# A hybrid decoder trunk on one core: holding the order of the output projections, dealing out the splits of y by weight tile, and moving one chunk of tokens to the second group

## The chip, the core and the metric

The kernel runs on one core of one Trainium2 chip. The core has five engines with an instruction stream each: TensorE (PE: matmuls, with weight loads shown as PEld), VectorE (DVE), ScalarE (ACT), GpSimd (POOL) and SyncE (SP), which here issues all the DMAs. An engine works through its stream in order and waits at an instruction until what it needs is there. The metric is the time of one launch in microseconds of the device, as a median over several runs.

## What is computed

Two layers of a hybrid trunk on 1040 tokens (16 meta tokens and 1024 of the sequence) of width 1024, all in float32:

```python
def hybrid_layer(x, ...):
    h = rms_norm(x, norm_g)
    z = h @ w_in                       # 1024 -> 6408, split in parts
    ya = sliding_window_sink_attention(...) * silu(ag)          # 16 heads, 2 KV heads
    ym = rms_norm(mlstm_chunkwise(...)) * sigmoid(mo) * silu(mgate)
    y = concatenate([ya, ym], -1) @ w_out                       # 2048 -> 1024
    return x + y
```

After the last layer the meta tokens are dropped.

## The kernel before

**Precision.** A float32 product is made of three matmuls in a faster format: each operand is split in a high part (`hi`, a rounded copy, made on ACT) and a low part (`lo`, the value less `hi`, made on DVE or POOL), and hi x hi, hi x lo and lo x hi are added in one PSUM bank. Weights come from DRAM into one of two `raw` buffers, and their parts go into one of the eight slots of a ring (`RING`). `wpair` (L147) does so for the input weights, `wout` (L168) for the output weights: a load on SP (L172), `hi` on ACT (L174), `lo` on DVE or POOL (L175).

**Stages of a layer.** K and V (`kv_tasks`), queries and gates woven with attention, the mLSTM heads woven with their projections, and the output projection, which ends the layer. In the first layer each finished token tile is then normalised and transposed into `H` for the next layer (`norm_tile`, L273). The order on PE is held by hand in the attention stage alone: `pin` (L65 ff.) ties a PE instruction behind the one traced before it while `in_order[0]` is true, and it is false in the output projection. Wherever it is false, and for every other engine always, the order of a stream is chosen by the scheduler at build time, from the order of tracing as priority and from simulated times; the chip then runs that fixed stream.

**The output projection** (L1087 to L1162). Its input y has 16 tiles of 128 features; 14 lie in DRAM (`spool`) and the last two made (`ym`, order positions 12 and 13) are still on chip. First a loop over all 16 tiles and all three chunks of tokens (`CH`: 272, 384 and 384 tokens) loads y (L1096) and splits it: `hi` into `H` on ACT (L1100), `lo` into `ylo` on DVE or on POOL for every third tile (L1105), and in layer 0 extra copies for the 16 meta tokens (L1102, L1103). Then four groups follow: token tiles 0 to 4 (in the last layer 1 to 4) with the left half of the columns of `w_out` and with the right half, then token tiles 5 to 8 with both halves. A group goes through the 16 weight tiles; each is multiplied with every token tile of the group (`product`, L1131), three matmuls of 512 columns each, or two for token tile 0, where 16 tokens are handled with a stacked operand. Every token tile of a group has its own PSUM bank, taken in turn from three pools with two banks each (`pj`, `pss`, `po`); a fourth pool, `pt`, also of two, takes transposes. The last group alone goes through its last eight weights tile by tile (`cut`).

When a token tile is done, DVE adds the residual out of the bank (L1153, for token tile 0 L1152 too). In the last layer the result goes to the output (L1155). In the first it is stored to `x1` in DRAM (L1157), and ACT takes the sum of its squares (L1158, whose unused result is written over the bank). After the right half, the left half is loaded back (L1161) and `norm_tile` follows: the factor on DVE and POOL (L277 to L279), the scaling on DVE (L285), eight transposes on PE (L288), and the parts into `H` on ACT and DVE (L291, L292).

**Buffers.** Loads of y alternate between the pool `p512` (4 buffers) and `t384` (5 buffers). The results, and the left halves loaded back, are in `p512` too.

Of the kernel before, what the change touches and what calls it, by code (L numbers as in the profile page):

```python
# [29 lines left out]
TT = [(0, 16)] + [(16 + 128 * i, 128) for i in range(8)]  # L30
CH = [(0, 272, range(0, 3)), (272, 384, range(3, 6)), (656, 384, range(6, 9))]
# [31 lines left out]
def build(ctx, tc, I, O):  # L63
# [4 lines left out]
    def pin(ins):  # L68

        return tc.keep_in_program_order(ins) if in_order[0] else ins  # L70
# [25 lines left out]
    def bank(tag):  # L96
        return bp[tag].tile([128, 512], F32, name=tag)
# [70 lines left out]
    def wout(l, k, c0, i):  # L168
        raw = rawp.tile([128, 2, 264], F32, name="raw").rearrange("p a b -> p (a b)")[:, 0:512]
        pair = RING[:, ring_i[0] % NPAIR]  # L170
        ring_i[0] += 1
        sy.dma_start(raw, I["w_out"][l][k * 128:(k + 1) * 128, c0:c0 + 512])  # L172
        hi, lo = [pair[:, a].rearrange("p a b -> p (a b)")[:, 0:512] for a in range(2)]
        sc.activation(hi, raw, AF.Copy)  # L174
        (ve if i % 3 == 2 else gp).tensor_tensor(lo, raw, hi, op=ALU.subtract)  # L175
        return hi, lo

    def mm3(out, pairs):
# [92 lines left out]
            done = upto  # L271


    def norm_tile(t, xh, ssq_ap, gbc):
        t0, p = TT[t]
        v = sm.tile([128, 2], F32, name="nv", bufs=2)
        ve.tensor_reduce(v[:p, 0:1], ssq_ap, axis=mybir.AxisListType.X, op=ALU.add)  # L277
        ve.tensor_scalar(v[:p, 0:1], v[:p, 0:1], 1.0 / D, EPS, ALU.mult, ALU.add)
        gp.tensor_tensor(v[:p, 1:2], v[:p, 0:1], nhalf[:p, 0:1], op=ALU.pow)  # L279
        for g in range(2):  # L280
            if gbc is None:
                ve.tensor_scalar(xh[g][:p, :], xh[g][:p, :], v[:p, 1:2], None, ALU.mult)
            for i in range(2 if gbc is not None else 0):
                xs = xh[g][:p, 256 * i:256 * i + 256]
                ve.scalar_tensor_tensor(xs, xs, v[:p, 1:2], gbc[2 * g + i][:p, 0:256], ALU.mult, ALU.mult)  # L285
            ps = bank("pt")
            for k in range(4):
                pin(pe.transpose(ps[:, k * p:(k + 1) * p], xh[g][:p, k * 128:(k + 1) * 128], ident[:p, :p]))  # L288
            src = ps[:, 0:4 * p].rearrange("p (k t) -> p k t", k=4)
            hi = H[:, 4 * g:4 * g + 4, t0:t0 + p]  # L290
            sc.activation(hi, src, AF.Copy)  # L291
            ve.tensor_tensor(H[:, 8 + 4 * g:12 + 4 * g, t0:t0 + p], src, hi, op=ALU.subtract)  # L292
            if t == 0:
                for i in range(3):
                    ve.tensor_copy(HM[:, 4 * g:4 * g + 4, 16 * i:16 * i + 16],
                                   H[:, 4 * (g + i // 2 * 2):4 * (g + i // 2 * 2) + 4, 0:16])

    def load_g(l):
        out = []
# [12 lines left out]
    def first_norm(t, xt, G):  # L312
        t0, p = TT[t]
        st = sm.tile([128, 2], F32, name="nst", bufs=2)
        xg = []
        for i in range(2):
            j = bank("pss") if i else bank("po")
            sc.activation(j[:p, :], xt[:p, 512 * i:512 * i + 512], AF.Square, accum_out=st[:p, i:i + 1])
            y = p512(F32)
            gp.tensor_tensor(y[:p, :], xt[:p, 512 * i:512 * i + 512], G[:p, 512 * i:512 * i + 512], op=ALU.mult)  # L320
            xg.append(y)
        norm_tile(t, xg, st[:p, 0:2], None)

    snk = cp.tile([128, 2, HEADS], F32, name="snk")
    qrt = cp.tile([128, 9, 32], F32, name="qrt")
# [18 lines left out]
    def parameters2(rows):  # L344
# [5 lines left out]
        for t in ptm:  # L350
            ve.tensor_scalar(t, ident, 0.0, None, ALU.mult)

    for l in range(DEPTH):
        last = l == DEPTH - 1
        first_q = 1 if last else 0
# [96 lines left out]
        def kv_tasks():  # L452
# [634 lines left out]
        order = list(range(0, 12)) + [14, 15, 12, 13]  # L1087
        s0 = N_META if last else 0
        ylo = {}
        for i, k in enumerate(order):  # L1090
            ylo[k] = unit(F32R)
            for c, (t0, n, _) in enumerate(CH):
                a = s0 if c == 0 else t0
                if k < 14:
                    y = p512(F32, t0 + n - a) if (i + c) % 2 else t384(t0 + n - a)
                    sy.dma_start(y, spool[k, :, a:t0 + n])  # L1096
                else:
                    y = ym[k - 14][:, a:t0 + n]
                hi = H[:, k, a:t0 + n]
                sc.activation(hi, y, AF.Copy)  # L1100
                if a == 0:
                    sc.activation(ylo[k][:, L:L + 32], y[:, 0:32], AF.Copy)  # L1102
                    gp.tensor_tensor(ylo[k][:, L + 32:L + 48], y[:, 0:16], ylo[k][:, L:L + 16], op=ALU.subtract)  # L1103
                eng = gp if i % 3 == 2 else ve
                eng.tensor_tensor(ylo[k][:, a:t0 + n], y, hi, op=ALU.subtract)  # L1105
# [5 lines left out]
        nb = 0  # L1111
        for grp in (range(first_q, 5), range(5, 9)):
            for hf in range(2):
                c0 = 512 * hf
                pss_t = {}
                for t in grp:
                    pss_t[t] = bank(pools[nb % 3])
                    nb += 1
                def product(i, k, t, w):
                    t0, p = TT[t]  # L1120
                    ps = pss_t[t]
                    wh, wl = w
                    if t == 0:
                        st = ylo[k][:, L:L + 48]
                        terms = ((st, wh), (st, wl))
                        p = 48
                    else:
                        hi, lo = H[:, k, t0:t0 + p], ylo[k][:, t0:t0 + p]
                        terms = ((hi, wh), (hi, wl), (lo, wh))
                    for n, (a, b) in enumerate(terms):  # L1130
                        pin(pe.matmul(ps[:p, :], a, b, start=(i + n == 0), stop=(i == 15 and n == len(terms) - 1)))  # L1131

                cut = 16 - 8 if hf == 1 and grp[-1] == 8 else 16
                for i, k in enumerate(order[:cut]):
                    w = wout(l, k, c0, i)
                    for t in grp:
                        product(i, k, t, w)
                tail = [(i, order[i], wout(l, order[i], c0, i)) for i in range(cut, 16)]
                for t in grp:
                    for i, k, w in tail:  # L1140
                        product(i, k, t, w)
                    t0, p = TT[t]
                    xr = p512(F32)
                    if l > 0:
                        src = x1[t0:t0 + p, c0:c0 + 512]
                    elif t == 0:
                        src = I["meta"][:, c0:c0 + 512]
                    else:
                        src = I["x"][t0 - 16:t0 + 112, c0:c0 + 512]
                    sy.dma_start(xr[:p, :], src)  # L1150
                    if t == 0:
                        ve.tensor_tensor(xr[:16, :], pss_t[t][32:48, :], xr[:16, :], op=ALU.add)  # L1152
                    ve.tensor_tensor(xr[:p, :], pss_t[t][:p, :], xr[:p, :], op=ALU.add)  # L1153
                    if last:
                        sy.dma_start(O["out"][t0 - 16:t0 + 112, c0:c0 + 512], xr[:p, :])  # L1155
                        continue
                    sy.dma_start(x1[t0:t0 + p, c0:c0 + 512], xr[:p, :])  # L1157
                    sc.activation(pss_t[t][:p, :], xr[:p, :], AF.Square, accum_out=ssq[:p, t, hf:hf + 1])  # L1158
                    if hf == 1:
                        x0 = p512(F32)  # L1160
                        sy.dma_start(x0[:p, :], x1[t0:t0 + p, 0:512])  # L1161
                        norm_tile(t, [x0, xr], ssq[:p, t, :], gbc)  # L1162


_INS = ("x", "meta", "norm_g", "w_in", "attn_q_norm_g", "attn_k_norm_g", "attn_sink",
# [17 lines left out]
```

## Time and profile before

| | |
|---|---|
| runs before | 2018.02, 2017.27 and 2020.26 us; median 2018.02 us |
| the profiled execution | 2017.04 us; its span from the first to the last instruction 2015.3 us |
| granted TensorE clock, mean over the span | 0.986 |
| DMA traffic | 122.01 MB read and 23.29 MB written, 72 GB/s over the span |
| matmuls of the output projections (L1131) | 842.1 to 1052 us in layer 0, 1823.8 to 2011.7 us in layer 1 |
| weights of the output projections | 128 loads of 256.0 KB, median 2.7 us from issue to landing |

The busy time of an engine is the sum over its instructions; matmuls are pipelined, and their ends are modelled. A wait is the idle time of an engine ahead of an instruction, and it is put down to what came last of the things that the instruction needed. The granted clock is the share of full speed at which TensorE was let run. "RING", "raw", "H", "u" (the units, `ylo` among them) and "p" (`p512`) are names of the program.

### The profile page before, as it was taken

To read this page: it belongs to the slowest core of one execution; us is meant where nothing else is said; L and a number is where in the kernel's file an instruction comes from. 1 tells how busy PE (TensorE), PEld (TensorE's weight loads), DVE (VectorE), ACT (ScalarE), POOL (GpSimd) and SP (SyncE) were. 2 spreads that over 40 slices of the span, in tenths; PEclk is the share of its full clock that TensorE was granted. 3 is DMA by queue.
4 is the path that set the end of the run, shared out by engine and by line. 5 is a ranking of instruction groups with operands and counts; after the bars stand their busy time and mean duration, and the time that the engine had idled before them with its cause. 6 is when DMAs were issued, how large, how long until landed. Compare 5 with 4: busy or idle time off the path is not lost. (4 is left out here: it accounts for less than half of the span.)

```text
span 2015.3 us, 36021 instructions
## 1 busy us (share of the span) xinstructions
PE 1926.3 (96%) x12823; PEld 1815.1 (90%) x12823; DVE 1151.2 (57%) x3037; ACT 1032.5 (51%) x3065; POOL 913.0 (45%) x1052
## 2 busy tenths in 40 slices
PE   6999899999999999999999999999999999999899
PEld 6999899989999999867889999999999999998787
DVE  7767767667556464531535678775673736547111
ACT  5567767745353434542334678776454434346221
POOL 7544544335454445552325345443355443547331
PEclk9999999999999999999999999999999999999999
DMA  5111111121212121453442111111122221216443
GB/s 159 43 35 43 39 41 37 36 61 35 56 47 61 40 61 57 127 168 124 158 148 55 47 35 53 42 40 53 38 57 61 44 63 45 55 51 220 151 141 105
DMA packets 149795, 147.71 MB, mean 73 GB/s; under 512 B 14952, under 2 KB 122768, under 8 KB 149616
## 3 DMA queue, kind: packets, MB, share of 16 engines
q1 hardware_dynamic: 149616, 145.41, 24.7%
q8 instruction: 101, 1.65, 0.3%
q14 instruction: 78, 0.64, 0.1%
HBM read 122.01 MB, written 23.29 MB: 72 GB/s over the span
## 5 line engine op out<-in xcount | busy, mean ns | idle before, releaser
L183 PE MATMUL pj<-H,RING 128*128 128x384 f32 (+2 forms) x3456 | 584.0, 325 | 9.2 <-ACT u L819 9.2
L183 PEld LDWEIGHTS pj<-H,RING 128*128 128x128 f32 x3456 | 551.8, 191 | 12.7 <-ACT u L819 10.3
L160 POOL TENSOR_TENSOR RING<-raw,RING 128x512 fp32r<-128x512 f32 (+1 forms) x196 | 261.1, 1341 | 135.2 <-ACT RING L159 116.4
L222 PE MATMUL pj<-RING,H 128*128 128x256 f32 (+1 forms) x1920 | 269.8, 287 | 1.9 <-DVE w1k L190 1.9
L222 PEld LDWEIGHTS pj<-RING,H 128*128 128x128 f32 x1920 | 243.8, 190 | 2.4 <-DVE w1k L190 2.2
L222 PE MATMUL pj<-H,RING 128*128 128x384 f32 (+2 forms) x1152 | 218.6, 328 | 2.6 <-DVE u L564 2.5
L183 PE MATMUL pj<-RING,H 128*128 128x256 f32 x1536 | 203.1, 286 | 2.1 <-DVE H L292 1.4
L175 POOL TENSOR_TENSOR RING<-raw,RING 128x512 fp32r<-128x512 f32 x88 | 115.2, 1313 | 195.2 <-ACT RING L174 191.8
L183 PEld LDWEIGHTS pj<-RING,H 128*128 128x128 f32 x1536 | 190.6, 190 | 3.5 <-DVE H L292 1.6
L222 PEld LDWEIGHTS pj<-H,RING 128*128 128x128 f32 x1152 | 181.4, 192 | 3.5 <-PE T L668 1.3
L174 ACT ACTIVATE RING<-raw 128x512 fp32r<-128x512 f32 x128 | 80.7, 632 | 201.0 <-DMA raw<-in_w_out_dram 131.7
L159 ACT ACTIVATE RING<-raw 128x512 fp32r<-128x512 f32 (+1 forms) x196 | 122.6, 629 | 70.4 <-DMA raw<-in_w_in_dram 45.7
L713 POOL TENSOR_TENSOR u<-u,w1k 128x128 f32<-128x128 f32 (+1 forms) x136 | 64.0, 471 | 178.2 <-DVE w1k L709 167.0
L175 DVE TENSOR_TENSOR RING<-raw,RING 128x512 fp32r<-128x512 f32 x40 | 31.6, 791 | 195.0 <-ACT RING L174 195.0
L649 ACT ACTIVATE t<-S,mx 128x145 f32<-128x145 f32 (+1 forms) x272 | 100.6, 374 | 63.7 <-DVE mx L646 56.9
L679 POOL TENSOR_SCALAR_AFFINE_SELECT p<-p 128x512 fp32r<-128x512 f32 x112 | 72.4, 646 | 133.1 <-DVE p L675 130.0
L878 POOL TENSOR_TENSOR p<-u,p 128x258 fp32r<-128x258 f32 x64 | 46.3, 723 | 175.3 <-ACT p L877 172.7
L1131 PE MATMUL pj<-RING,H 128*128 128x512 f32 x352 | 113.4, 402 | 6.9 <-DVE p L1153 6.1
L824 DVE SCALAR_TENSOR_TENSOR t<-u,cw,t 128x384 f32<-128x384 f32 (+1 forms) x144 | 118.7, 824 | 2.2
L1131 PE MATMUL pss<-RING,H 128*128 128x512 f32 x352 | 113.6, 402 | 1.8 <-ACT H L1100 0.9
L628 PE MATMUL S<-u 128*128 128x272 f32 (+2 forms) x544 | 87.6, 280 | 19.3 <-DVE u L563 16.6
L654 ACT ACTIVATE t<-t,mx 128x144 f32<-128x144 f32 (+1 forms) x272 | 97.6, 406 | 14.9 <-DVE mx L651 14.6
(342 smaller groups left out, 3832.4 us busy)
## 6 DMA issues: line engine op xcount, KB each, us to landing
raw<-in_w_out_dram SPq DMA_DIRECT2D x128, 256.0 KB, 2.7
raw<-in_w_in_dram SPq DMA_DIRECT2D x100, 256.0 KB, 2.8
raw<-in_w_in_dram SPq DMA_DIRECT2D x192, 128.0 KB, 2.3
spool<-u SPq DMA_DIRECT2D x56, 192.0 KB, 1.9
p<-x SPq DMA_DIRECT2D x24, 256.0 KB, 4.2
t<-spool SPq DMA_DIRECT2D x28, 192.0 KB, 3.7
p<-spool SPq DMA_DIRECT2D x28, 192.0 KB, 3.8
u<-em SPq DMA_DIRECT2D x8, 576.0 KB, 6.6
```

The lines of the kernel that those rows point to most:

```text
L159: sc.activation(hi, raw[:, :, 0:o], AF.Copy)
L160: eng.tensor_tensor(lo, raw[:, :, 0:o], hi, op=ALU.subtract)
L174: sc.activation(hi, raw, AF.Copy)
L175: (ve if i % 3 == 2 else gp).tensor_tensor(lo, raw, hi, op=ALU.subtract)
L183: pin(pe.matmul(out, a, b, start=(i == 0), stop=(i == n - 1)))
L222: pin(pe.matmul(out(), x, y, start=(k + i == 0), stop=(k == n - 1 and i == 2)))
L628: pin(pe.matmul(S[:p, h, o + 2 - 2 * h:o + 2 - 2 * h + kn], lq, Ks[i][:, k0:k0 + kn], start=(i == 0), stop=(i == 1)))
L649: sc.activation(P[:p, 145 * h:145 * h + 145], S[:p, h, 1 + 127 * h:146 + 127 * h], AF.Exp, bias=mx[:p, 0, h:h + 1], accum_out=mx[:p, 1, h: ...
L654: sc.activation(Pn, Pn, AF.Copy, scale=mx[:p, 2, h:h + 1])
L679: gp.affine_select(OW, HL, [[0, 4], [1, 128]], ALU.is_ge, 0.0, base=0, channel_multiplier=-1)
L824: ve.scalar_tensor_tensor(z, RAW[:, t0 + i:t0 + i + n], wcol(i), z, ALU.mult, ALU.add)
L1131: pin(pe.matmul(ps[:p, :], a, b, start=(i + n == 0), stop=(i == 15 and n == len(terms) - 1)))
```

## The change

1. `wout`: `lo` of a weight is made on DVE for the positions 9, 11, 13 and 15 of a group (before: 2, 5, 8, 11 and 14), and on POOL otherwise.
2. `norm_tile` is cut in two: `norm_pre` (factor and scaling) and `norm_half` (four transposes and the two parts into `H`, for one half of the features).
3. The loop that splits y is gone. `y_split(i, c)` does one tile and chunk. In the first group it is called for chunks 0 and 1 just ahead of each weight, in the second for chunk 2. The last chunk's tokens are first read in the third group.
4. PE's order is held (`in_order`) from the second group to the fourth. The first three groups go through their last three weights tile by tile, the fourth through its last six (before: none, and eight in the fourth).
5. The sum of squares writes its unused result to `pt`, not to the bank of the token tile. The banks are taken as two of `pj`, two of `pss`, two of `po`.
6. The norm of the token tiles 0 to 4 is moved to the third group (`norm_again`, which loads both halves back from `x1`); `turn` places one half's transposes after each of the weights 3 to 12. Those of the tiles 5 to 8 are placed between the tiles of the fourth group, with the left half loaded in two pieces of `t384`; what is left (three halves) is handed to the next layer's K and V loop (`carry`).

```diff
-        (ve if i % 3 == 2 else gp).tensor_tensor(lo, raw, hi, op=ALU.subtract)
+        (ve if i > 8 and i % 2 else gp).tensor_tensor(lo, raw, hi, op=ALU.subtract)
...
-    def norm_tile(t, xh, ssq_ap, gbc):
+    def norm_pre(t, xq, ssq_ap, gbc):
...
+    def norm_half(t, g, xs):
...
                 ps = projN(wg, t, 256)
+                if l > 0 and t != 1 and carry:
+                    carry.pop(0)()
...
-        for i, k in enumerate(order):
-            ylo[k] = unit(F32R)
-            for c, (t0, n, _) in enumerate(CH):
...
+        def y_split(i, c):
...
-        pools = ["pj", "pss", "po"]
+        pools = ["pj", "pj", "pss", "pss", "po", "po"]
...
+            sc.activation(bank("pt")[:p, :], xr[:p, :], AF.Square, accum_out=ssq[:p, t, hf:hf + 1])
...
+        def norm_later(t, xq):
+            norm_pre(t, xq, ssq[:TT[t][1], t, :], gbc)
+            turns.extend(lambda g=g: norm_half(t, g, xq[2 * g:2 * g + 2]) for g in range(2))
+
+        def norm_again(t):
+
+            t0, p = TT[t]
+            x = [p512(F32) for _ in range(2)]
+            for i in range(2):
+                sy.dma_start(x[i][:p, :], x1[t0:t0 + p, 512 * i:512 * i + 512])
+            norm_later(t, [y[:, o:o + 256] for y in x for o in (0, 256)])
+
+        def turn(least=1):
+            if len(turns) >= least:
+                turns.pop(0)()
+
+        for g, (grp, hf) in enumerate([(grp, hf) for grp in (range(first_q, 5), range(5, 9)) for hf in range(2)]):
+            c0 = 512 * hf
+            in_order[0] = g > 0
+            pss_t = {}
+            for t in grp:
+                pss_t[t] = bank(pools[nb[0] % 6])
+                nb[0] += 1
+            cut = 10 if g == 3 else 13
+            chunks = ((0, 1), (2,), (), ())[g]
+            for i in range(cut):
+                for c in chunks:
+                    y_split(i, c)
+                w = wout(l, order[i], c0, i)
                 for t in grp:
+                    product(pss_t[t], i, t, w)
+                if g == 2 and not last:
+                    if i > 2:
+                        turn()
+                    if i % 2 and i < 10:
+                        norm_again(i // 2)
+            for i in range(cut, 16):
+                for c in chunks:
+                    y_split(i, c)
+            tail = [(i, wout(l, order[i], c0, i)) for i in range(cut, 16)]
+            for t in grp:
+                for i, w in tail:
+                    product(pss_t[t], i, t, w)
+                    if g == 3 and i == 12:
+                        turn(3)
+                if g == 3:
+                    turn(2)
+                result(pss_t[t], t, hf)
+        in_order[0] = False
+        carry[:] = turns
```

More of the change, by code (lines that the diff above doesn't have):

```diff
@@ L351, in parameters2 @@
             ve.tensor_scalar(t, ident, 0.0, None, ALU.mult)
+    carry = []
     for l in range(DEPTH):
@@ L1109, in build @@
             gbc = load_g(l + 1)
-        pools = ["pj", "pss", "po"]
[L1111 to L1115, printed above, removed]
-                for t in grp:
[L1117 to L1162, printed above, removed]
@@ new lines, in build, with product @@
+        pools = ["pj", "pj", "pss", "pss", "po", "po"]
+        nb = [0]
+        turns = []
+        def product(ps, i, t, w):
+            k = order[i]
+            t0, p = TT[t]
+            wh, wl = w
+            if t == 0:
+                st = ylo[k][:, L:L + 48]
+                terms = ((st, wh), (st, wl))
+                p = 48
+            else:
+                hi, lo = H[:, k, t0:t0 + p], ylo[k][:, t0:t0 + p]
+                terms = ((hi, wh), (hi, wl), (lo, wh))
+            for n, (a, b) in enumerate(terms):
+                pin(pe.matmul(ps[:p, :], a, b, start=(i + n == 0), stop=(i == 15 and n == len(terms) - 1)))
@@ new lines, in result @@
+        def result(ps, t, hf):
+            t0, p = TT[t]
+            c0 = 512 * hf
+            xr = p512(F32)
+            if l > 0:
+                src = x1[t0:t0 + p, c0:c0 + 512]
+            elif t == 0:
+                src = I["meta"][:, c0:c0 + 512]
+            else:
+                src = I["x"][t0 - 16:t0 + 112, c0:c0 + 512]
+            sy.dma_start(xr[:p, :], src)
+            if t == 0:
+                ve.tensor_tensor(xr[:16, :], ps[32:48, :], xr[:16, :], op=ALU.add)
+            ve.tensor_tensor(xr[:p, :], ps[:p, :], xr[:p, :], op=ALU.add)
+            if last:
+                sy.dma_start(O["out"][t0 - 16:t0 + 112, c0:c0 + 512], xr[:p, :])
+                return
+            if hf == 1 and t > 4:
+                x0 = [t384(256) for _ in range(2)]
+                for i, x in enumerate(x0):
+                    sy.dma_start(x[:p, :], x1[t0:t0 + p, 256 * i:256 * i + 256])
+            sy.dma_start(x1[t0:t0 + p, c0:c0 + 512], xr[:p, :])
+            sc.activation(bank("pt")[:p, :], xr[:p, :], AF.Square, accum_out=ssq[:p, t, hf:hf + 1])
+            if hf == 1 and t > 4:
+                norm_later(t, x0 + [xr[:, 0:256], xr[:, 256:512]])
```

68 lines of the change are left out of this document (38 added, 30 removed).

## Prediction

> **What bounds the kernel now.** I read the page first (busy shares, slices), then the waits of TensorE (PE) in the two output projections, then windows cut around each wait, and last the chain of waits at the longest one. From the page:
>
> ```profile
> span 2015.3 us, 36021 instructions
> PE 1926.3 (96%) x12823; PEld 1815.1 (90%) x12823; DVE 1151.2 (57%) x3037; ACT 1032.5 (51%) x3065; POOL 913.0 (45%) x1052
> ```
>
> PE works for 96% of the span, so an edit that leaves the number of matmuls alone can win only what PE idles or runs slowly. The change touches the output projections: about 842 to 1052 us in layer 0, 1824 to 2012 us in layer 1. The waits of PE there (us in total, times, longest), the last row from layer 1:
>
> ```profile
> PE pj L1131 <- POOL RING L175: 1.9, 1, 1.9
> PE po L1131 <- ACT RING L174: 1.5, 2, 1.1
> PE pss L1131 <- ACT H L1100: 0.9, 1, 0.9
> PE pss L1131 <- ACT pss L1158: 0.9, 1, 0.9
> PE pt L288 <- DVE H L292: 0.9, 1, 0.9
> PE pj L206 <- POOL RING L160: 0.3, 1, 0.3
> PE po L1131 <- DVE RING L175: 0.3, 1, 0.3
> PE pj L1131 <- DVE p L1153: 6.1, 1, 6.1
> ```
>
> Few waits, but the clock falls with them. In the windows (length, then busy us of PE, PEld, DVE, ACT, POOL with counts, granted clock, DMA share, GB/s):
>
> ```profile
> 842.00:846.00 4.00, 3.93 (x12) 2.90 (x13) 3.92 (x10) 4.00 (x16) 3.63 (x6) 0.57 0.99 330
> 874.00:881.00 7.00, 5.11 (x16) 3.57 (x15) 0.86 (x2) 1.17 (x2) 5.21 (x9) 0.76 0.60 190
> 900.00:911.00 11.00, 8.32 (x27) 4.96 (x26) 3.85 (x6) 4.82 (x12) 4.01 (x4) 0.84 0.55 178
> 911.00:1052.00 141.00, 141.00 (x639) 113.46 (x638) 45.97 (x95) 42.11 (x83) 42.13 (x37) 1.00 0.43 138
> 1052.00:1061.00 9.00, 7.72 (x62) 7.01 (x61) 6.70 (x14) 4.37 (x10) 4.93 (x5) 1.00 0.51 157
> 1872.00:1884.30 12.30, 6.17 (x18) 4.60 (x17) 3.09 (x5) 3.54 (x6) 5.05 (x4) 0.72 0.49 155
> 1884.30:2011.70 127.40, 127.37 (x549) 102.69 (x548) 16.62 (x24) 24.91 (x40) 34.97 (x27) 1.00 0.40 130
> ```
>
> A window costs its idle time plus (1 - clock) x length of slow running. Five losses, and clean stretches between them (141.00 of 141.00 us; 127.37 of 127.40):
> **S**, the start of layer 0's projection: 0.9 waited for the first H, then 0.43 x 4 = 1.7; 2.6 us.
> **C**, inside the first group: 7.00 - 5.11 = 1.9 idle, 0.24 x 7 = 1.7 slow; 3.6 us.
> **B**, first to second group of layer 0: 11.00 - 8.32 = 2.7 idle, 0.16 x 11 = 1.8 slow; 4.5 us.
> **E**, into layer 1: 9.00 - 7.72 = 1.3 us.
> **A**, first to second group of layer 1: 12.30 - 6.17 = 6.1 idle; its slow part I count in the chain, as the window's 0.72 covers idle time too:
>
> ```profile
> 1876.88 0.64 ACT RING L174
> 1877.54 0.04 DVE RING L175
> 1878.15 0.69 DVE p L1153
> 1878.89 1.65 PE pj L1131 x3
> 1880.54 1.28 PE pss L1131 x3
> 1881.82 1.28 PE pj L1131 x3
> 1883.10 1.19 PE pss L1131 x4
> 1891.22 1.39 PE pss L1131 x6
> ```
>
> A full-speed matmul is 1.39 / 6 = 0.232 us. The 13 after the wait take 1.65 + 1.28 + 1.28 + 1.19 = 5.4 us for 3.0: 2.4 lost, so A is 8.5 us. The chain tells why: the banks of the first group had to be emptied by L1153 on VectorE (DVE), but the scheduler had put a weight split (L175) ahead of it on DVE, and that split waited for its weight's DMA and for ACT.
>
> All five together are 2.6 + 3.6 + 4.5 + 1.3 + 8.5 = 20.5 us: the most that the output projections can give back.
>
> **The change, part by part.**
>
> *Splits of y dealt out by weight tile.* Now all 48 pieces (16 tiles of y, 3 chunks; 42 are loaded) are traced ahead of any weight of the projection. What that does in layer 0, on the SP and POOL queues:
>
> ```profile
> 858.40 2.64 SPq L1096 DMA_DIRECT2D t<-spool  x4
> 864.50 0.43 SPq L172 DMA_DIRECT2D raw<-in_w_out_dram  x1
> 873.72 1.30 POOL L1105 TENSOR_TENSOR u<-p,H 128x384 fp32r<-128x384 f32 x1
> 874.99 1.26 POOL L175 TENSOR_TENSOR RING<-raw,RING 128x512 fp32r<-128x512 f32 x1
> ```
>
> The first weight after the prefetched ones is asked for at 864.50, behind nearly all loads of y, and its split stands behind POOL's last split of y; PE waits for it: loss C. After the change 28 loads instead of 42 fall in the first group, each pair just ahead of its own weight in priority, and 14 go to the second. I take all of C off: -3.6 (bounds 0 and 3.6). S waits for the first load of y, which is still first: 0.
>
> What the 14 loads cost in the second group is not shown; the rows for its bounds (the last two are the landing times of the weights and of the loads of y):
>
> ```profile
> L174 ACT ACTIVATE RING<-raw x58: 612/633/637, 839.6 to 1030.3; 128x512 fp32r<-128x512 f32 x58
> L175 POOL TENSOR_TENSOR RING<-raw,RING x40: 1258/1292/1652, 840.4 to 1031.1; 128x512 fp32r<-128x512 f32 x40
> L175 DVE TENSOR_TENSOR RING<-raw,RING x18: 680/693/1266, 869.4 to 1029.5; 128x512 fp32r<-128x512 f32 x18
> DMA to landing us min/median/max: 2.5/2.7/4.3
> DMA to landing us min/median/max: 2.3/3.7/5.1
> ```
>
> A weight holds one of two raw buffers for 2.7 + 0.63 + 1.29 = 4.6 us, so one comes every 2.3 us. PE uses one in 12 x 0.232 = 2.8 us with four token tiles, 14 x 0.232 = 3.2 with five. If the loads of y stretch the landing to 3.7, it is 5.6 / 2 = 2.8: no margin in layer 1, but a lead of three to five weights to use up first. Bounds: 0, and a stall like C in each layer (7.2). I take 1.0, near the lower end because of the lead: +1.0. That POOL has 12 of 16 splits instead of 11 adds 0.6 us a group to an engine that is 45% busy: 0.
>
> *Order held from the second group on, a tail of three weights.* The last three weights go tile by tile, so the first tile ends early: its bank is emptied (0.69) while the others run at 9 x 0.232 = 2.1 us each. With six banks in turn, the tightest reuse (layer 0, the fifth tile of the second group on the fourth tile's bank) comes 2.1 + 0.5 + 3 x 0.7 = 4.7 us after that tile's end, the others later. L175 is on DVE only for tiles 9, 11, 13 and 15, so no early weight of the next group can stand ahead of L1153, and Square (L1158) writes to pt, not into the bank PE waits for. The waits of A and B lose their cause. If a split of y takes L175's place on DVE, L1153 may still be 4.7 - 0.7 = 4.0 us late before PE notices. I take both off: -8.5 and -4.5 (bounds 0 and all).
>
> *The norm moved.* The 72 transposes stay. For tiles 0 to 4 both halves of x1 are read back in the third group: five loads more, and two half loads for one in tiles 5 to 8; nine more issues on SP. They sit at fixed places in PE's stream, so a late one stops PE. Rows for the chain:
>
> ```profile
> 1035.64 0.69 DVE L1153 TENSOR_TENSOR p<-po,p 128x512 f32<-128x512 f32 x1 [5.47 <-PE po L1131]
> 1038.13 1.67 DVE L285 SCALAR_TENSOR_TENSOR p<-p,nv,w1k 128x256 f32<-128x256 f32 x4 [0.67 <-POOL nv L279]
> p<-x SPq DMA_DIRECT2D x24, 256.0 KB, 4.2
> SPq L172 <- POOL RING L175: 55.0, 31, 3.4
> ```
>
> Tile 5's first half is ready half of 1.67 after 1038.13, at 1039.0: 3.4 us after its bank. Its turn comes after tile 6's tail, 18 x 0.232 = 4.2 us: it fits by 0.8. In the third group, tile t+2's buffers are freed by tile t's transposes and needed four weights, 11.2 us, later; a load (4.2), half of the scaling (0.8) and a longest SP wait (3.4) make 8.4. It fits by 2.8. Cost 0; its end is the third rival.
>
> *Last group's tail six instead of eight weights, three halves of the norm carried into layer 1.* Two ring slots come free for layer 1's first weights, and the transposes stand among K/V matmuls: most of E goes, -1.0 (0 to 1.3).
>
> **Sum**: -3.6 - 4.5 - 8.5 - 1.0 + 1.0 = -16.6 us. The profiled execution took 2017.0 us (span 2015.3 and 1.7 around it), so 2000.4; the median of the runs shown, 2018.0, lies 1.0 above it, so 2001.4.
>
> [...]
>
> **The rivals.**
> 1. *Weights late in the second group.* For: 2.8 against 2.8 us in layer 1. Against: the lead, and layer 0's 3.2. A stall like C in both layers gives 2001.4 - 1.0 + 7.2 = 2007.6. Chance 0.16.
> 2. *DVE still late at the switch.* The order on DVE is still the scheduler's; a split of y waiting for its load can stand ahead of L1153. A stays: 2001.4 + 8.5 = 2009.9; B too: 2014.4. Against: several us of slack. Chance 0.12.
> 3. *Slower: the fixed transposes wait.* Place: third group of layer 0, tiles 2, 3 and 4. If a load of x1 stands behind weight DMAs that wait for raw buffers, the round takes more than 11.2 us and PE stops three times, each with some 1.7 of slow clock. At 16.8 us a round: 3 x (5.6 + 1.7) = 21.9, so 2023.3. It turns slower than before from 16.6 / 3 - 1.7 = 3.8 us a stop, a round of 15. Against: 8.4 us from the rows, longest SP wait included. Chance 0.10.
> 4. *The change doesn't do what it says.* Only PE is held, and the first group not at all; the other queues may come out as now, and the switches with them: about 2017. Chance 0.05.
> 5. *Short waits cost no clock*, so that the slow parts of B and C have another cause and stay: 2004.9. [...] Chance 0.03.
>
> **How the numbers follow.** The forecast has the remaining 0.54, and its own range is 1997 (all 20.5 gone) to 2005 (E stays, one C-like stall). Likeliest is its time, 2001.4. Runs of this kernel cannot tell less than 0.2%, 4 us, from no change. Faster by more: forecast, rivals 1 and 5, and most of 2: 0.83. Within: rival 4 and the rest of 2: 0.07. Slower: rival 3: 0.10. The range 1997 to 2012 takes in the forecast, rivals 1 and 5 and the better part of 2: about 0.8.
>
> **What would show it.** Right: no PE wait over 0.5 us and a clock of 1.00 at the four group switches; no wait for RING in layer 0's first group; S unchanged; L1153 on DVE within 1 us of its tile's last matmul. Wrong: PE waiting for RING in a second group (rival 1), for L1153 (rival 2), or transposes waiting for DVE or for x1 (rival 3). A shift of some us in stages that the diff doesn't touch, as the scheduler lays out the whole program anew, would make the total wrong with every step right.

## The result, and the profile after

| | before | after |
|---|---|---|
| median of the runs | 2017.64 us (2016.51 to 2020.26) | 2004.85 us (2003.56 to 2006.05) |
| ratio, after over before | | 0.9934, 95% interval 0.9919 to 0.9949 |
| profiled execution, its span | 2017.04, 2015.3 us | 2006.05, 2003.9 us |

The kernel is faster by 12.8 us by its medians; the forecast was 16.6. The page of the changed kernel (line numbers are its own from here on: `product` is L1139, the residual's load L1152, its sum L1155, the output's store L1157, the load of y L1109, its splits L1113 to L1118):

```profile
span 2003.9 us, 36035 instructions
PE 1920.3 (96%) x12823; PEld 1807.3 (90%) x12823; DVE 1149.3 (57%) x3029; ACT 1032.0 (51%) x3065; POOL 921.1 (46%) x1060
```

The span is 11.4 us shorter with the same 12823 matmuls, and PE's busy time has shrunk by only 6.0: the rest was idling. The windows of the changed kernel, cut where before had its losses and where new waits showed (columns as in the prediction):

```profile
842.00:846.00 4.00, 3.83 (x18) 2.73 (x18) 3.48 (x12) 3.27 (x12) 2.76 (x6) 1.00 0.89 269
846.00:904.00 58.00, 58.00 (x254) 44.69 (x253) 26.90 (x42) 29.31 (x74) 37.47 (x45) 1.00 0.63 196
904.00:1044.00 140.00, 140.00 (x643) 111.93 (x642) 49.70 (x94) 46.06 (x91) 50.09 (x44) 1.00 0.52 161
1044.00:1057.00 13.00, 11.29 (x86) 10.12 (x85) 10.91 (x20) 5.99 (x14) 6.03 (x6) 1.00 0.38 103
1856.00:1870.00 14.00, 14.00 (x62) 11.30 (x61) 1.85 (x3) 3.47 (x6) 5.43 (x5) 1.00 0.55 168
1870.00:1960.00 90.00, 90.00 (x389) 72.83 (x388) 13.74 (x20) 23.30 (x38) 34.29 (x27) 1.00 0.49 153
1960.00:1985.00 25.00, 22.15 (x86) 16.11 (x85) 2.77 (x4) 5.69 (x9) 6.37 (x5) 0.95 0.45 139
1985.00:1992.00 7.00, 7.00 (x23) 5.53 (x23) 0.88 (x2) 0.00 (x0) 0.00 (x0) 0.70 0.10 37
```

C and B lay in the second row and at its end: PE is busy in 58.00 of 58.00 us, and its clock is 1.00. A lay in the fifth: 14.00 of 14.00. All three are gone. At S, which the forecast left as it was, the clock is 1.00 where it was 0.57, and PE's waits for H and for the unit behind it are short (waits in layer 0's projection, changed kernel):

```profile
PE pss L1139 <- ACT H L1113: 0.3, 1, 0.3
...
PE pss L1139 <- DVE u L1118: 0.2, 1, 0.2
```

E is not better: 13.00 - 11.29 = 1.7 us idle, against 1.3. And there is a new loss, in the last group of layer 1, the last two rows: 25.00 - 22.15 = 2.85 idle, 0.05 x 25 = 1.25 and 0.30 x 7 = 2.1 slow, together 6.2 us. PE's waits in layer 1's projection, changed kernel (us in total, times, longest):

```profile
PE pj L1139 <- POOL RING L175: 1.5, 3, 0.8
PE po L876 <- DVE w1k L938: 1.1, 1, 1.1
PE pj L1139 <- ACT RING L174: 1.0, 1, 1.0
...
PE pj L1139 <- DVE RING L175: 0.2, 1, 0.2
```

The second row stands in both kernels (it ends just ahead of the projection). The others are waits for weights, 2.7 us together. The queues tell why. First ACT in the changed kernel's timeline (start, us, engine and line, and in brackets the idle time before it and what ended it): each row is the high part of one weight.

```profile
1955.91 0.64 ACT L174 ACTIVATE RING<-raw 128x512 fp32r<-128x512 f32 x1 [2.55 <-DMA raw<-in_w_out_dram]
1966.20 1.28 ACT L174 ACTIVATE RING<-raw 128x512 fp32r<-128x512 f32 x2 [9.65 <-DMA raw<-in_w_out_dram]
```

For 9.65 us no weight came. Then the chain of waits of the changed kernel over that gap:

```profile
1952.91 0.33 SPq L172
...
1953.29 3.21 DMA out_dram<-p
1956.52 0.33 SPq L1152
...
1956.89 0.43 SPq L1157
...
1957.36 3.50 DMA out_dram<-p
1960.88 0.33 SPq L1152
...
1961.31 0.38 SPq L1157
...
1961.78 4.31 DMA raw<-in_w_out_dram
```

SP issues the stores of the third group's results (L1157), and between them the residual loads of the last group (L1152). Such a load needs a `p512` buffer, there are four, and a store holds it until its DMA of 3.2 to 3.5 us is done. So SP stands at L1152 twice in this stretch, and the weights (L172), which need no `p512`, stand behind it from 1952.9 to 1961.8. The lead covers the gap; the tail of six weights that follows, one for each 3 x 0.232 = 0.7 us of the first tile, is what uses the lead up.

The kernel before had this cover, as its SP timeline shows:

```profile
1935.84 27.52 SPq L172 DMA_DIRECT2D raw<-in_w_out_dram  x12
1965.79 0.34 SPq L1155 DMA_DIRECT2D out_dram<-p  x1
```

Twelve weights in a row, and the first store of the third group's results only behind them.

### The profile page after: what moved, and what is told of

It is laid out like the page before. It is cut to its first block, busy times and chain, and to the rows that moved or that the text cites. A ratio compares the mean times of both kernels' runs of the same rounds, so it can differ in the third digit from the quotient of the medians.

```text
span 2003.9 us, 36035 instructions
## 1 busy us (share of the span) xinstructions
PE 1920.3 (96%) x12823; PEld 1807.3 (90%) x12823; DVE 1149.3 (57%) x3029; ACT 1032.0 (51%) x3065; POOL 921.1 (46%) x1060
## 4 chain that ended last, share of the span: by engine, by line
PE 65%; DVE 12%; DMA 6%; POOL 6%; issue 5%; ACT 5%; SPq 0%; POOLq 0%; ACTq 0%; DVEq 0%
PE pj L183 27%; PE pj L222 15%; PE pss L1139 4%; PE pj L1139 4%; DMA raw<-in_w_out_dram 3%; PE po L1139 3%; DVE t L833 3%; PE S L637 3%; PE O L713 2%; DMA raw<-in_w_in_dram 2%; POOL RING L175 2%; PE po L876 2%; POOL RING L160 2%; PE O L701 1%; PE T L677 1%
## 5 line engine op out<-in xcount | busy, mean ns | idle before, releaser
L175 POOL TENSOR_TENSOR RING<-raw,RING 128x512 fp32r<-128x512 f32 x96 | 125.3, 1311 | 185.7 <-ACT RING L174 177.6
L174 ACT ACTIVATE RING<-raw 128x512 fp32r<-128x512 f32 x128 | 80.8, 632 | 183.9 <-DMA raw<-in_w_out_dram 156.5
L1139 PE MATMUL pss<-RING,H 128*128 128x512 f32 x384 | 120.2, 394 | 0.3 <-ACT H L1113 0.3
L1139 PE MATMUL pj<-RING,H 128*128 128x512 f32 x352 | 113.4, 403 | 3.2 <-POOL RING L175 1.5
L175 DVE TENSOR_TENSOR RING<-raw,RING 128x512 fp32r<-128x512 f32 x32 | 24.3, 761 | 125.1 <-ACT RING L174 125.1
```

The lines of the kernel that those rows point to most:

```text
L175: (ve if i > 8 and i % 2 else gp).tensor_tensor(lo, raw, hi, op=ALU.subtract)
```

## The experiments

Two lengths from the traces serve beside the medians, as they repeat better and leave out the stages ahead, which took 840.9 us in one profile of the changed kernel and 836.9 in the other: **X**, from PE's first matmul after the 1.1 us wait for L938 (L929 in the kernel before) just ahead of layer 0's projection to the same matmul in layer 1, and **Y**, from there to the end of PE's last matmul. X holds S, C, B and E (and all of layer 1 up to its projection), Y holds A and the last group. Two profiles of the changed kernel give 971.8 and 973.1 for X and 187.4 and 185.9 for Y; before has 981.9 and 189.2. Every kernel below computes the whole result.

| kernel | median, us | ratio to before, 95% | X | Y |
|---|---|---|---|---|
| after | 2004.85 | 0.9934 (0.9919 to 0.9949) | 971.8 | 187.4 |
| late | 1998.44 | 0.9908 (0.9875 to 0.9940) | 971.8 | 181.7 |
| cut13 | 1996.53 | 0.9901 (0.9880 to 0.9923) | 972.1 | 180.3 |
| b_deal | 2016.25 | 0.9999 (0.9988 to 1.0009) | 982.7 | 190.8 |
| b_y | 2000.45 | 0.9913 (0.9889 to 0.9937) | 970.9 | 186.1 |
| b_one | 2012.37 | 0.9985 (0.9972 to 0.9997) | 977.7 | 189.6 |
| b_c2 | 2010.66 | 0.9978 (0.9966 to 0.9990) | 977.5 | 190.4 |
| notail | 1996.47 | 0.9898 (0.9872 to 0.9924) | 973.9 | 180.2 |
| free13 | 2004.32 | 0.9932 (0.9909 to 0.9955) | 976.6 | 184.8 |
| after2 (after again) | 2004.84 | 0.9954 (0.9940 to 0.9969) | 973.1 | 185.9 |
| cut13b (cut13 again) | 2001.47 | 0.9936 (0.9920 to 0.9951) | 971.5 | 180.1 |
| olddeal13 | 2001.74 | 0.9936 (0.9922 to 0.9949) | 975.9 | 182.6 |
| b_y_deal | 1999.01 | 0.9927 (0.9912 to 0.9942) | 975.8 | 181.6 |

late to b_y were measured on one chip, b_one to free13 on a second, the last four on a third. One kernel's ratio moved by 0.0020 (after) and 0.0035 (cut13) between chips, 4 and 7 us: only rows of one chip are compared by medians.

### The new loss: the order on SP, or the tail

late (after, with the last group's four residual loads ahead of its tail in the program and held there on SP):

```diff
+            early = {t: residual(t, hf) for t in grp} if last and g == 3 else {}
             for t in grp:
...
-                result(pss_t[t], t, hf)
+                result(pss_t[t], t, hf, early.get(t))
```

> The changed kernel, with the four residual loads of the last group of the last layer traced ahead of that group's tail and tied on SP behind its last weight load. Queue theory (in the changed kernel three residual loads and the stores that they wait for stand on SP ahead of weights 7 and 8 of that group, ACT gets no weight for 9.65 us, and the tail of six weights then comes too early): the waits of PE for RING in that tail go, 2.7 us of idling and some 3 us of slow clock, so about 5.5 us less than the changed kernel's 2004.9, 1999.4, ratio to before 0.991; ACT gets a weight every 2 to 3 us. Rate theory (two raw buffers give a weight every 2.3 to 2.6 us, and a tail that takes one every 0.7 us starves whatever stands on SP): no change, 2004.9, ratio 0.9937, PE waits for RING as before.

cut13 (after, with a tail of three in the last group of the last layer):

```diff
-            cut = 10 if g == 3 else 13
+            cut = 10 if g == 3 and not last else 13
```

> The changed kernel, with a tail of three weights instead of six in the last group of the last layer. Queue theory and rate theory both: weights 10 to 12 are now needed every 2.8 us instead of every 0.7, so PE no longer waits: about 5.5 us less than 2004.9, 1999.4. The two differ in the trace: by the queue theory the gap of some 9 us on ACT before weight 7 stays, hidden by the ring. If PE still waits there, the tail is not what turned the late weights into a stall.

In late, SP issues the stores and all weights, and the residuals behind them (SP's timeline, late; its L1166 is the store, L1151 the residual's load):

```profile
1949.78 1.44 SPq L1166 DMA_DIRECT2D out_dram<-p  x3
...
1954.38 16.63 SPq L172 DMA_DIRECT2D raw<-in_w_out_dram  x8
1971.06 1.85 SPq L1151 DMA_DIRECT2D p<-x  x4
```

ACT's longest gap between weights falls from 9.65 to 2.91 us, PE's waits in the last group from 2.7 to 0.9, and Y by 5.8 us. cut13 leaves SP as it was, and ACT's timeline still has the gap:

```profile
1959.81 1.31 ACT L174 ACTIVATE RING<-raw 128x512 fp32r<-128x512 f32 x2 [9.21 <-DMA raw<-in_w_out_dram]
```

Yet PE waits for no weight there, and Y falls by 7.2: a whole round of four tiles takes 2.8 us a weight and lives off the lead. In the changed kernel the loss thus takes both, the gap on SP and the tail of six: without either one most or all of it goes. A tail of three is no safeguard by itself, as free13 shows below.

### Why C, B and A went: DVE's weight splits, or the loads of y

The prediction had two causes: weights queued behind y on SP (C), and a weight split on DVE ahead of L1153 (A, B). b_deal is the kernel before with the new deal of weight splits alone:

```diff
-        (ve if i % 3 == 2 else gp).tensor_tensor(lo, raw, hi, op=ALU.subtract)
+        (ve if i > 8 and i % 2 else gp).tensor_tensor(lo, raw, hi, op=ALU.subtract)
```

> The kernel before, with the low parts of the weights dealt to DVE as in the change (positions 9, 11, 13, 15), nothing else. Theory of the prediction (loss A came from a weight split of the next group standing on DVE ahead of the additions that empty the banks): A goes, 8.5 us, and B loses its 0.3 us behind DVE; about 2009, ratio 0.9955. Rival (it is the tail by tiles that lets the banks be emptied in time): A stays in the main, 2015 to 2018.

No gain: 0.9999, where the prediction's theory expected 0.9955. The waits at the switches of both layers, A and B, are gone, but others came in their place, in the first group of each layer (PE's timeline, b_deal):

```profile
869.13 0.63 PE L1131 MATMUL pj<-RING,u 128*48 128x512 f32 x1 [4.69 <-POOL u L1105]
...
1848.72 0.80 PE L1131 MATMUL pj<-RING,H 128*128 128x512 f32 x1 [6.97 <-ACT RING L174]
```

In layer 0 a wait of 4.69 us for a split of y on POOL stands in place of C's 1.89 for a weight. In layer 1 A's 6.1 us at 1878 became 6.97 at 1848, and there it is a late weight: what came last is its high part on ACT (RING, L174). b_y is the kernel before with the splits of y dealt out by weight tile and the third chunk in the second group, and nothing else: a function `y_split(i, cs)` in place of the loop, and

```diff
+                    if grp[-1] == 4:
+                        y_split(i, ((0, 1), (2,))[hf])
```

ahead of each weight.

> The kernel before, with the splits of y dealt out as in the change (chunks 0 and 1 ahead of each weight of the first group, chunk 2 ahead of each weight of the second), nothing else. Theory of the prediction (loss C came from weights queued behind all loads of y on SP and behind its splits on POOL): C goes, 3.6 us; the start S, which fell from 2.6 to some 0.5 us with the whole change, may go too; A and B stay: 2012 to 2014, ratio 0.997 to 0.998. Rival (C came from the share of POOL in the weight splits, or the loads of y collide with weights in the second group): no gain, 2017 or more.

It gains 11.0 in X and 3.2 in Y, ratio 0.9913, with no order held, no tail, the old deal and the old norm: far more than the 0.997 to 0.998 expected, as B went too. On SP its first weight of the projection behind loads of y is asked for at 847.31, before at 864.50 (SP's timeline, b_y):

```profile
847.31 0.42 SPq L172 DMA_DIRECT2D raw<-in_w_out_dram  x1
```

PE waits for no weight in layer 0's projection. At A a wait of 3.52 us is left and 1.7 of slow clock behind it, 5.2 us of the 8.5. It has the chain that the prediction gave for A, in short form (chain of waits, b_y; its L1158 is the sum of L1153):

```profile
1860.77 0.64 ACT RING L174
...
1861.43 0.04 DVE RING L175
...
1862.04 0.69 DVE p L1158
...
1862.78 0.96 PE pj L1134 x3
```

In DVE's timeline of b_y, DVE stands idle at that weight split, with the additions of all four tiles behind it:

```profile
1861.43 0.69 DVE L175 TENSOR_TENSOR RING<-raw,RING 128x512 fp32r<-128x512 f32 x1 [7.44 <-ACT RING L174]
```

b_one deals all three chunks out in the first group; b_c2 deals nothing out and only moves the third chunk's loop ahead of the second group. b_one has

```diff
+                    if grp[-1] == 4 and hf == 0:
+                        y_split(i, (0, 1, 2))
```

and b_c2

```diff
+                if grp[-1] == 4:
+                    for i in range(16):
+                        y_split(i, ((0, 1), (2,))[hf])
```

> The kernel before, with the splits of y dealt out ahead of each weight of the first group, all three chunks there (nothing moved to the second group). Theory (weights come too late because the loads and splits of y are traced, and so served, ahead of all of them; what counts is that each weight gets its turn among them): most of what dealing out in two groups gave (15.6 us, 0.9913) is here too; no wait for RING in the first group of layer 0, ratio 0.992 to 0.995. Rival (what counts is the third chunk's 14 loads, 2.7 MB, taken out of the crowded first group): a stall like C stays, and with it late weights at the switches; ratio 0.997 to 1.000.

> The kernel before, with only the third chunk moved: chunks 0 and 1 are loaded and split in one go ahead of the first group, chunk 2 in one go ahead of the second, nothing dealt out by weight. Theory (each weight needs its turn): C is smaller, as 28 instead of 42 loads stand ahead of weight 8, but the second group's weights now stand behind 14 loads: some stall at the switches; ratio 0.995 to 0.999. Rival (the third chunk's place is what counts): nearly the whole gain of dealing out in two groups, ratio 0.991 to 0.993.

Each takes C away (X 4.2 and 4.4 us shorter) and leaves B and A. PE's timeline of b_one:

```profile
897.24 0.43 PE L1134 MATMUL po<-RING,u 128*48 128x512 f32 x1 [1.08 <-ACT RING L174]
...
1871.45 1.22 PE L1134 MATMUL pj<-RING,H 128*128 128x512 f32 x2 [5.93 <-DVE p L1158]
```

b_c2 has waits at the same two places, the longest of 1.32 and 7.34 us. By ratio b_one missed the range of its theory (0.9985 for 0.992 to 0.995), and b_c2 met it. Neither the dealing nor the split over two groups is the cause alone: either by itself gives some 4.3 us in X and nothing in Y, both together 14.2. In b_one 42 loads still share the first group with 16 weights, in b_c2 a block of loads still stands ahead of each group's weights.

### The held order and the tails of three

notail is cut13 with no tail in the first three groups:

```diff
-            cut = 10 if g == 3 and not last else 13
+            cut = 16 if g < 3 else 13 if last else 10
```

free13 is cut13 with PE's order nowhere held in the projection:

```diff
-            in_order[0] = g > 0
+            in_order[0] = False
```

> The changed kernel with a tail of three in the last group of the last layer (1996.5 us, 0.9901), and no tail in the first three groups: all 16 weights go through all token tiles, order still held. Theory now (weights on time are enough in layer 0; in layer 1 dealing out alone left a wait of 3.5 us and 1.8 of slow clock for an addition behind a weight split on DVE, which the new deal of the splits avoids): within 2 us of 1996.5, ratio 0.990 to 0.992. The prediction's step (the tail by tiles lets the banks be emptied in time): waits for L1155 at the switches of both layers, 0.7 to 3 us each with slow clock behind them, up to 10 us more, ratio 0.993 to 0.995.

> The changed kernel with a tail of three in the last group of the last layer (1996.5 us, 0.9901), and PE's order never held in the projections. Theory now (with the weights on time, the scheduler's own order is as good, and nearly the same): no change, ratio 0.989 to 0.992, the same waits of PE within 1 us. The prediction's step (the held order takes away the waits at the switches): waits for L1155 or for banks come back, A and B, up to 13 us, ratio up to 0.9965.

notail has no wait at any switch, and its ratio is within the noise of cut13's on the other chip (0.9898 and 0.9901). free13 has clean switches too, but X is 4.5 and Y 4.6 us longer than in cut13. Its losses lie elsewhere. It runs layer 1's first matmuls ahead and then waits at the layer's start, and its last group waits 2.1 and 0.9 us for RING, in spite of the short tail. PE's timeline of free13:

```profile
1048.50 5.26 PE L183 MATMUL pj<-RING,H 128*128 128x256 f32 x24 [4.23 <-ACT u L498]
```

The wait in the last group comes with the gap in the supply of weights, here a little longer than in cut13. ACT's timeline of free13:

```profile
1970.06 1.27 ACT L174 ACTIVATE RING<-raw 128x512 fp32r<-128x512 f32 x2 [10.75 <-DMA raw<-in_w_out_dram]
```

What holding PE's order is worth here is thus not the switches it was charged to, but the layer's start. Whether it also keeps the lead that covers the gap in the last group, or SP's order alone decides that, is not shown.

### Either deal, on one chip

olddeal13 is cut13 with the old deal of weight splits, b_y_deal is b_y with the new one (the diff of b_deal, or its reverse).

> The changed kernel as it is, once more beside the others on one chip: 0.9934 to 0.9937 of the kernel before by its first measurement, 6 to 8 us slower than with the shorter last tail, all of it in the last group of the last layer.

> The changed kernel with a tail of three in the last group of the last layer once more, beside the others on one chip: 0.990 as before. Against the two-part version it says what held order, tails and the moved norm are worth with the weights on time: by the theory nothing, a difference below 0.2%.

> The changed kernel with a tail of three in the last group of the last layer, and the weight splits dealt to DVE as before (positions 2, 5, 8, 11, 14). Theory: at the first switch of layer 1 the scheduler still puts a split of the next group ahead of one of the additions, but with the tail the tiles end one after another and the weights come in time; a wait of 0 to 3.5 us, ratio 0.990 to 0.992 against 0.990 with the new deal. If the deal alone carried that switch, the full 5.3 us come back, ratio 0.9925 or more.

> The kernel before, with the splits of y dealt out in two groups and the new deal of the weight splits to DVE, and nothing else of the change (no held order, no tail by tiles, the norm as before). Theory (what dealing out alone left in layer 1, a wait of 3.5 us and 1.8 of slow clock, is a weight split of the second group standing on DVE ahead of the additions; with the new deal the first such split of a group is its tenth): that wait goes, 5.3 us less than dealing out alone (0.9913), ratio 0.988 to 0.990, as fast as the changed kernel with the shorter last tail. Rival (held order or tail is needed for that switch): the wait stays, ratio 0.991 to 0.992.

By ratio all four came out above what was expected of them (0.9954, 0.9936, 0.9936 and 0.9927), on a chip where the kernel before was faster (2014.54 us, for 2016 to 2018 on the others). The ratio of olddeal13 even lies where its rival put it, so the traces have to tell. after2 shows the last group's stall again (waits for RING of 0.22, 1.11 and 0.85 us), cut13b none, and in X and Y together after2 is 7.4 us longer, by medians 3.4 (6 to 8 were expected). A's rest of b_y, 3.52 us, is in neither b_y_deal nor olddeal13. The window over that switch in b_y:

```profile
1856.00:1872.00 16.00, 12.47 (x48) 9.67 (x47) 4.18 (x7) 4.15 (x7) 5.11 (x4) 0.89 0.60 191
```

The same window in b_y_deal:

```profile
1856.00:1872.00 16.00, 16.00 (x71) 12.94 (x70) 2.70 (x4) 3.80 (x6) 7.77 (x6) 1.00 0.46 150
```

So once y is dealt out, the new deal suffices for it, and so does the rest of the change without the new deal. b_y_deal has a little of B instead (0.75 and 0.91 us at 894, and 1.7 of slow clock) and a last group's wait of 0.84.

The deal also turned out to set the wait at S. SP's timeline at the start of layer 0's projection in olddeal13:

```profile
835.95 0.88 SPq L172 DMA_DIRECT2D raw<-in_w_out_dram  x2
836.88 0.90 SPq L1109 DMA_DIRECT2D t<-spool  x2
```

And in cut13b:

```profile
837.60 0.33 SPq L172 DMA_DIRECT2D raw<-in_w_out_dram  x1
837.98 0.90 SPq L1109 DMA_DIRECT2D t<-spool  x2
```

With the old deal SP issues two weights ahead of y, with the new one a single weight. PE's wait for the first H in layer 0 was 0.90 (before), 0.83 (b_y) and 0.87 us (olddeal13) with the old deal, and 0.39 (b_deal), 0.28 (b_y_deal) and 0.18 (cut13b) with the new one: three pairs that differ in this line alone. Why the scheduler then issues the second weight later was not tried. The slow clock behind S goes with it only in part: all five profiles with the old deal lost clock there (0.67 to 0.72 over 5 us from the end of the 1.07 us wait ahead of the projection), and of the nine with the new one three (late, notail and b_deal: 0.68, 0.71 and 0.73) still did. In olddeal13 the layer 0 projection is 2.7 us longer than in cut13b, some 2.2 of it at S, the rest a transpose's wait of 0.56 us for DVE in the third group; the other 1.7 us of its longer X lie between the two projections, in stages that no edit touches. Of the nearly 5 us by which X of b_y_deal exceeds that of b_y, 1.9 are in the projection (S gained less than the rest of B cost), 1.8 at layer 1's start, where a wait of 1.91 us for DVE had slow clock behind it (0.93 from 1036 to 1060 us) and one of 0.93 us in b_y had none (1.00 over the same window), and 1.2 in the stages behind.

By medians cut13b, olddeal13 and b_y_deal lie 3 to 6 us ahead of after2 (2001.47, 2001.74 and 1999.01 against 2004.84), and each one's runs spread over 3 to 10 us: which of the three is fastest stays open. (In X and Y together cut13b is the shortest, some 6 us below b_y_deal, whose median is the lowest.) b_y_deal is the smallest of them, two edits to the kernel before.

## Why the prediction was right, and where it was off

The time of 2004.85 us lies in the range, and 3.5 above the likeliest value. By time alone rivals 1 (2007.6) and 5 (2004.9) lie nearer than the forecast, so the traces decide. The sum of -16.6 us against -11.4 in the spans, -12.8 in the medians and -11.9 in X and Y together, by its own terms:

| term | forecast | measured | |
|---|---|---|---|
| C | -3.6 | -3.6 | 846 to 904: 58.00 of 58.00 us, clock 1.00 |
| B | -4.5 | -4.5 | the same window and the start of the next |
| A | -8.5 | -8.5 | 1856 to 1870: 14.00 of 14.00 us, clock 1.00 |
| E | -1.0 | +0.4 | 1.7 us idle for 1.3 |
| S | 0 | -2.1 | layer 0: 0.3 + 0.2 us waited and no slow part, for 2.6; the slow part, 1.7, partly by luck |
| weights late | +1.0, second groups | +6.2, last group of layer 1 | 2.85 idle, 3.35 slow |
| sum | -16.6 | -12.1 | |

**Mis-sized: the late weights.** The term stood at 1.0, for the loads of y that move to the second group. There they cost nothing (90.00 of 90.00 and 140.00 of 140.00 us busy). The stall came two groups later, from stores and residual loads on the same queue. The prediction counted the moved DMAs of the norm past SP in layer 0, but listed the last groups of layer 1 as a clean stretch (127.37 of 127.40 us before) and gave them no term, though it wrote of rival 4 that the other queues may come out anew. A tail of six that lives off a lead of weights was never priced. Rival 1 named the symptom, PE waiting for RING, in the wrong group and for the wrong reason. That the total still came out near is in part luck: the gain of 2.1 at S, forecast as 0, made up for a third of that stall.

**Right in size, half right in the cause.** A and B were put down to the weight split on DVE and to Square in the bank, C alone to the weights behind y. For B the loads of y were enough: b_y, which keeps the old deal, no tail and Square in the bank, has no wait at that switch. For A both were needed. Dealing out y alone took 3.3 of the 8.5 us; what it left is the split on DVE, as predicted, and goes when the split is moved as well (b_y_deal) or when the rest of the change is there without the new deal (olddeal13). Moving the split alone (b_deal) took the wait at the switch away and brought one as long inside the first group. So the chain of waits was read correctly, but its first link, the weight that came late, counted as much as the split behind it. The tail of three was given a part in A and B too; notail shows that it needs none.

**Off by little.** E: the halves of the norm carried into layer 1 wait there themselves. PE's timeline of the changed kernel:

```profile
1048.65 0.66 PE L292 MATMUL pt<-cst,p 128*128 128x128 f32 x4 [0.23 <-ACT pt L1164]
...
1054.07 0.66 PE L292 MATMUL pt<-cst,p 128*128 128x128 f32 x4 [0.66 <-DVE H L296]
```

S: the prediction looked at the load of y, still the first of its kind; what changed is that one weight instead of two stands ahead of it. Two small slips changed nothing: the list of losses leaves out layer 1's own start (0.7 us for its first H, 0.3 after the change), and one more split a group on POOL is 1.29 us, not the 0.6 by which POOL is slower than DVE.

**The other rivals.** Rival 2 was closer than the total shows. DVE's timeline of the changed kernel at layer 1's first switch:

```profile
1853.02 0.69 DVE L1155 TENSOR_TENSOR p<-pj,p 128x512 f32<-128x512 f32 x1 [3.10 <-PE pj L1139]
1855.18 0.69 DVE L1155 TENSOR_TENSOR p<-pj,p 128x512 f32<-128x512 f32 x1 [1.47 <-PE pj L1139]
...
1867.89 0.56 DVE L1118 TENSOR_TENSOR u<-p,H 128x384 fp32r<-128x384 f32 x1 [10.00 <-ACT H L1113]
1868.36 0.68 DVE L1155 TENSOR_TENSOR p<-pss,p 128x512 f32<-128x512 f32 x1
```

A split of y stood ahead of the fourth tile's sum and waited for 10.00 us, as rival 2 had it, and the mark "L1153 within 1 us" was missed. It cost nothing because the second group uses the banks of the first two tiles (`pj`), which DVE had emptied at once; the fourth tile's is not needed before the third group. Rival 3 did not come in the changed kernel: the transposes placed in the third and fourth group of layer 0 lie in the window with 140.00 of 140.00 us busy. Rival 4 did not either, though free13 shows that much of the gain needs no held order. Rival 5's time, 2004.9, is nearly the measured one, by chance: the slow parts of C and B went with their waits.

## What to carry to other kernels

When a wait is removed from a queue that one scheduler lays out, look at the whole queue in every later group: in the changed kernel two residual loads that waited for a buffer held back the weights behind them, which need no such buffer, from 1952.9 to 1961.8 us. Before a tail that takes several weights at once, check the producer's longest gap: with one of 9.65 us PE waited 2.7 us in a tail of six, with one of 9.21 not at all in cut13's tail of three. When a wait ends with one instruction, follow the chain back: here moving that instruction alone only moved the wait (6.1 us at 1878, then 6.97 at 1848). And try the cheap half of a large change by itself: here the dealing of the loads over two groups, some ten lines, gained as much as the whole change as it stands (X and Y together 1157.0 us, for 1159.2; before 1171.1).

## What the runs showed of the hardware

At S, C and B the kernel before lost clock in pieces of nearly one size. In the windows (1 - clock) x length was 0.43 x 4 = 1.7 us at S, 0.24 x 7 = 1.7 at C and 0.16 x 11 = 1.8 at B. Cut into windows of 1 us from 876 to 881, C's clock is 0.80, 0.50, 0.50, 0.50 and 0.99, which costs 0.20 + 3 x 0.50 + 0.01 = 1.7. The last group of the changed kernel lost twice that, 0.05 x 25 + 0.30 x 7 = 3.35 us. The wait just ahead of the slow clock was 0.90 us at S, for the first H, and 1.89 at C, for a weight.

Not every such wait was followed by a slow clock. Just ahead of layer 1's projection PE waits 1.07 or 1.08 us and a little later for the first H: 0.73 us in the kernel before, 0.72 in b_one, 0.81 in b_y, 0.90 in b_c2 and 1.10 in olddeal13. Only olddeal13 lost clock there: 0.72 over the 6 us from the end of the first wait, and 1.00 in the other four. That window in olddeal13:

```profile
1815.34:1821.34 6.00, 4.90 (x16) 3.95 (x17) 5.04 (x11) 5.47 (x17) 5.27 (x6) 0.72 0.91 294
```

And in the kernel before:

```profile
1822.47:1828.47 6.00, 5.27 (x24) 4.28 (x25) 5.90 (x14) 5.58 (x17) 4.49 (x5) 1.00 0.95 312
```

At S it is not the length of the wait alone that decides: after nearly the same waits (0.15 and 0.17 us in cut13, 0.21 and 0.17 in late, each behind one of 1.07) the clock over 5 us was 1.00 in the one and 0.68 in the other. What else has a part in it was not tried. The window of cut13:

```profile
836.12:841.12 5.00, 4.68 (x21) 3.37 (x22) 4.66 (x12) 4.36 (x16) 3.53 (x6) 1.00 0.87 272
```

And that of late:

```profile
836.90:841.90 5.00, 4.61 (x14) 3.17 (x15) 3.24 (x9) 3.79 (x14) 3.50 (x6) 0.68 0.82 260
```

That the format of the three matmuls of a product is faster than plain float32 was not measured here.
